# When weight low parts, side work and the modulation stream are issued in a two-layer diffusion backbone on one Trainium2 core

## The chip, the cores and the metric

The kernel runs on one core of a Trainium2 chip. The engines named below are TensorE (PE in the profile; PEld is its weight load), VectorE (DVE), ScalarE (ACT), GpSimd (POOL) and SyncE (SP, which here only issues transfers). The metric is the device time of one execution in microseconds; the median of several runs is given.

## The reference, cut to what matters

One inference step of two layers over 640 tokens of width 1024: 128 context tokens and 512 latent tokens, with the same weights and two modulation vectors.

```python
mod = silu(cond) @ w_ada + b_ada -> shift1, scale1, gate1, shift2, scale2, gate2
h = rmsnorm(x, g_pre_mix) * (1 + scale1) + shift1
z = h @ w_in                       # all branches and their gates
# A: GLU -> depthwise conv 31 -> LayerNorm -> swish;  B: pooling of 2/4/8/16 tokens
# C: b * depthwise conv 3 (c * h);  D: attention of +-128 tokens, latents also read a cache
merged = sum(sigmoid(gate_b) * (branch_b @ w_b_out) for b in "ABCD")
x += gate1 * rmsnorm(merged @ w_o, g_post_mix)
h = rmsnorm(x, g_pre_ffn) * (1 + scale2) + shift2
x += gate2 * rmsnorm(relu(h @ w_ff1)**2 @ w_ff2, g_post_ffn)
```

All is float32. The kernel splits each operand of a large product into a high part that TensorE multiplies fast and a low part (the rest), and sums three products of them.

## The kernel before, in words

The program is written out by Python in one order, and each engine works off its own instructions in that order. TensorE's products give the order its frame; everything else is put between them.

**Weights.** The weights come as 264 units of 128 x 1024, 132 a layer, in the order of use: 6 for q, k, v, 12 for the sections that feed the branches, then the four branches C, B, A, D with their gates (units 18 to 60), 8 for w_o, 64 for the feed-forward part. `w_next` takes the next unit and calls `w_pump` for up to 3 units ahead; `w_done` frees units and pumps again. `w_pump` (L126) issues for a unit the high part on ScalarE (L135), the low part on VectorE (L136), and the transfer of the raw unit three further on (L149, on SP's queue). There are 4 sets of high and low parts and 3 raw buffers.

**Side work.** Attention, branches A, B and C and the modulation are generators (`attention`, `post_a`, `pool_b`, `post_c`, `ada`) that issue a step of work and yield its cost in microseconds of VectorE. After about every half product group the frame calls `tick(pe, dve)` (L70): the TensorE time that has passed, less VectorE's fixed work, is added to a credit with a cap, and each generator in order of its rank gets one step while there is credit. A yield of 0.1 is a lag: a step that issues nothing, so that the next comes a tick later. `drain` issues all that is left of a generator at once. `zsplit` drains a branch before its product begins: C after the first pooling section, B, A and attention inside the last unit of the gates of the branch before.

**Modulation.** `mod_first` makes the first table. The rest is made by `ada`, in chunks of 512 columns: eight pairs of operations on VectorE (L380, L382) that multiply a piece of w_ada by a column of silu(cond) for both vectors, then two all-reductions over partitions on GpSimd (L394). For a gate (2 chunks) the result is multiplied by g_post (L421); for shift and scale (4 chunks) it goes through DRAM into the column tables `mc` (two transfers, L404 and L407), from which `make_ab` makes the tables A and B (L350 to L352). A layer's generator of gate 1 and the second column table is added at the start of its mixer and drained before w_o; that of gate 2 and the next layer's first column table is added before the feed-forward part and drained at the end of it.

**End of a mixer.** `natural` multiplies by w_o in two halves of four units, five token tiles each. In the second half a `Chain` normalises the tiles, adds them to x and makes the next h, with A and B from `ch.start()`. `run` says

```python
self.drain("ada")
ch = Chain(self, f, res[l, "gt1"], xs, lambda t: x1[t], res[l, "ab2"])
ch.start()
self.natural(mhi, mlo, f, "copy", ch)
```

Of the kernel before, what the change touches and what calls it, by code (L numbers as in the profile page):

```python
# [12 lines left out]
L = 2  # L13
# [8 lines left out]
T_BUFS = 26  # L22
# [4 lines left out]
RANK = dict(C=0, B=0, att=1, A=2, ada=3)  # L27
NAT_TICK = ((1.2, 0), (0.9, 0), (0.1, 0), (0.6, 0.6))
FF_DVE = 0.8
KN = {'ws': 0.2, 'l_brow': 2, 'l_red': 2, 'l_red2': 2, 'l_q': 2, 'l_last': 3, 'l_mean': 3, 'l_var': 3, 'l_rb': 4, 'l_ub': 2, 'sec': 0.5, 'gp': 0.1, 'bp': 0.5, 'qs': 2.0, 'qkv': 0, 'j0': -2, 'pv': 0.5, 'sc': 0.5, 'cv': 1.5}  # L30
PE_SCALE, CAP = 1.0, 2.5
W_DVE = 1.2
# [28 lines left out]

class Kernel:
# [19 lines left out]

# [6 lines left out]
    def add(self, name, gen, rank):  # L89
        self.sides.append((rank, name, gen))  # L90
        self.sides.sort(key=lambda s: s[0])

    def drain(self, *names):
        for s in list(self.sides):
            if not names or s[1] in names:
                for _ in s[2]:
                    pass
                self.sides.remove(s)

# [18 lines left out]
    def w_init(self):  # L118
        self.w_dma = 0
        self.w_split = 0  # L120
        self.w_at = 0
        self.w_live = 0
        self.w_raw = {}
        self.w_set = {}

    def w_pump(self, upto):  # L126
        nc = self.nc
        total = L * N_UNITS
        while self.w_split <= min(upto, total - 1) and self.w_live < N_SETS:
            i = self.w_split  # L130
            self.w_fetch(i)
# [4 lines left out]
            nc.vector.tensor_tensor(lo, raw, r32(hi), ALU.subtract)  # L136
            self.credit -= W_DVE
            self.w_set[i] = (hi, lo)
            self.w_split += 1
            self.w_live += 1  # L140
            self.w_fetch(i + N_RAW)

    def w_fetch(self, upto):
        while self.w_dma <= min(upto, L * N_UNITS - 1):
            i = self.w_dma
            if len(self.w_raw) >= N_RAW:
                break
            raw = self.wp.tile([128, 1024], F32, tag="wr", name=self.nm("wr"), bufs=N_RAW)
# [97 lines left out]
    def mod_first(self):  # L246
# [80 lines left out]
        self.w_pump(0)  # L327
        turn(1)
        self.w_pump(1)
        next(norm[0])  # L330
# [5 lines left out]
        self.w_pump(2)  # L336
        self.w_pump(3)
        for i in range(3):
# [24 lines left out]
    def ada_chunk(self, l, ch, red):  # L363
# [5 lines left out]
        for k in range(-3, 8):  # L369
# [13 lines left out]
            yield 1.2  # L383
# [40 lines left out]
    def ada(self, jobs, res):  # L424
        for l, j in jobs:
            if j == "gt1" or j == "gt2":
                G = [self.gpool.tile([128, D], F32, tag=f"G{c}", name=self.nm("G"), bufs=1) for c in range(2)]
                res[l, j] = G
                yield from self.ada_gate(l, 2 if j == "gt1" else 5, G)
            else:  # L430
# [5 lines left out]
                res[l, j] = (mc[0], mc[1], "sh" + n, "sc" + n, "g_pre_mix" if n == "1" else "g_pre_ffn")  # L436
# [91 lines left out]
    def natural(self, hi, lo, f, mode, ch=None):  # L528
# [5 lines left out]
        for n in range(2):  # L534
# [8 lines left out]
            if n == 1 and ch:  # L543
                us = [self.w_next() for _ in range(4)]
                for t in range(NT):
                    ps = self.mmps("nat")
                    for j in range(4):
# [10 lines left out]
                        elif j == 2:  # L558
                            ch.s2b(t - 1)
                    if mode == "add":  # L560
# [4 lines left out]
                self.w_pump(self.w_at + 1)  # L565
                return
# [199 lines left out]
    def post_a(self, us, z):  # L766
        nc = self.nc
        acc = []
        for i in range(2):
# [3 lines left out]
            for k in range(31):  # L773
# [7 lines left out]
                c += 0.8  # L781
# [124 lines left out]
    def mixer(self, l, hi, lo, mhi, mlo):  # L906
# [28 lines left out]
        self.add("att", self.attention(l, kvs, qns), RANK["att"])  # L935

        def section(fn):
            u, st = self.w_next()
            for h in range(2):
# [3 lines left out]
                self.tick(1.63, KN['sec'])  # L943
# [41 lines left out]
        self.add("A", self.post_a(ua, za), RANK["A"])  # L985
# [9 lines left out]
        self.add("C", self.post_c(uc, sb, zc), RANK["C"])  # L995

        ub = []
        for i in range(2):
# [10 lines left out]
            if i == 0:  # L1009
                nz = zsplit("C")  # L1010
        self.add("B", self.pool_b(l, ub, zb), RANK["B"])
# [3 lines left out]
        for bi, br in enumerate("CBAD"):  # L1015
# [3 lines left out]
            for f in range(8):  # L1019
# [9 lines left out]
                for h in range(2):  # L1029
# [7 lines left out]
                    self.tick(1.63, KN['gp'])  # L1037
# [5 lines left out]
                for h in range(2):  # L1043
# [14 lines left out]
                    self.tick(0.41 * nk, KN['bp'])  # L1058
# [4 lines left out]
    def ffn(self, hi, lo, f, ch):  # L1063
        nc = self.nc
        for c in range(4):
# [17 lines left out]
            for i, h in order:  # L1083
# [6 lines left out]
                self.tick(1.63, FF_DVE)  # L1090
# [6 lines left out]
    def run(self):  # L1097
# [3 lines left out]
        with tc.tile_pool(name="cp", bufs=1) as self.cp, tc.tile_pool(name="lp", bufs=1) as self.lp, \  # L1101
# [18 lines left out]
            res = {}  # L1120
            for l in range(L):
                self.layer_tables(l)
                self.add("ada", self.ada([(l, "gt1"), (l, "ab2")], res), RANK["ada"])
# [3 lines left out]
                with tc.tile_pool(name="xp", bufs=1, **SB) as self.xp:  # L1127
                    f = [self.xp.tile([128, D], F32, tag=f"f{t}", name=self.nm("f"), bufs=1) for t in range(NT)]
                    self.drain("ada")
# [3 lines left out]
                    self.natural(mhi, mlo, f, "copy", ch)  # L1133
                    hi, lo = ch.h
                    self.pend = ch.rest(0)
                    f = [self.xp.tile([128, D], F32, tag=f"f{t}", name=self.nm("f"), bufs=1) for t in range(NT)]
                    self.add("ada", self.ada([(l, "gt2")] + ([(l + 1, "ab1")] if l + 1 < L else []), res), RANK["ada"])
                    ch = Chain(self, f, None, lambda t: x1[t], (lambda t: x2[t]) if l + 1 < L else self.x_out, None)

                    def start(ch=ch, l=l):  # L1140
                        self.drain("ada")
                        ch.G = res[l, "gt2"]
                        if l + 1 < L:
                            self.layer_cols(l + 1)
# [4 lines left out]
                    self.ffn(hi, lo, f, ch)  # L1149
                    self.pend = ch.rest(1)  # L1150
# [7 lines left out]
class Chain:  # L1158
# [177 lines left out]
```

## Time and profile before

| | us |
|---|---|
| median of 3 runs | 2117.81 (2117.01 to 2119.41) |
| the profiled execution | 2116.92 |
| its span, first to last instruction | 2115.0 |
| TensorE busy in the span | 2034.1 |
| mean granted clock of TensorE, share of full | 0.984 |

The span is 1.9 us shorter than the execution that it is from. The profile shows one execution: for each engine the time that instructions ran, and for the idle time in front of an instruction what it waited for last. In rows of the timeline the first two numbers are the start and the duration, and brackets hold the idle time before and the instruction that ended it.

### The profile page before, as it was taken

The numbers are of one execution on the slowest core, as the hardware profiler recorded it, in microseconds if no ns is written. First come the engines' busy times: TensorE is split into PE (matmuls) and PEld (weight loads), VectorE is DVE, ScalarE is ACT, GpSimd is POOL, SyncE is SP. The second block draws the span as 40 slices with busy tenths as digits, with TensorE's granted clock in tenths as the row PEclk, the third lists the DMA queues.
The fourth block names the chain that finished last, engine by engine and source line by source line (L and its number), as shares of the span: only waits on it lengthen the run. The fifth ranks groups of instructions, "written<-read, shape, count | busy, mean of one in ns | idle before, by whom it ended". The sixth has DMA issues, their size and how long they took to land.

```text
span 2115.0 us, 30666 instructions
## 1 busy us (share of the span) xinstructions
PE 2034.1 (96%) x12354; PEld 1883.7 (89%) x12354; DVE 1314.5 (62%) x2306; ACT 788.7 (37%) x1540; POOL 283.0 (13%) x214
## 2 busy tenths in 40 slices
PE   8999998999699999999999999999996999999998
PEld 4999997999589898989889989989995989989896
DVE  6668766676677364754476768675784855333344
ACT  5434444442173241313354344454323633323131
POOL 1202000102321012220021020001132211000000
PEclk9999999999899999999999999999998999999999
DMA  8322221233434333332343112222443432222232
GB/s 302 116 69 68 71 67 57 84 110 130 137 143 132 116 120 120 110 120 70 119 140 103 61 64 80 68 84 71 133 132 127 157 118 92 84 78 72 80 100 80
DMA packets 77934, 221.40 MB, mean 105 GB/s; under 512 B 11224, under 2 KB 12248, under 8 KB 77792
## 3 DMA queue, kind: packets, MB, share of 16 engines
q1 hardware_dynamic: 48736, 165.32, 23.0%
q10 hardware_dynamic: 27520, 54.03, 7.7%
q8 instruction: 96, 1.57, 0.3%
q0 software_dynamic: 1536, 0.10, 0.3%
q14 instruction: 46, 0.38, 0.1%
HBM read 208.61 MB, written 10.80 MB: 104 GB/s over the span
## 4 chain that ended last, share of the span: by engine, by line
PE 77%; DVE 11%; ACT 5%; issue 2%; POOL 2%; DMA 2%; SPq 0%; ACTq 0%; DVEq 0%; POOLq 0%
PE nat L174 8%; PE nat L173 8%; PE nat L175 8%; PE ff L178 7%; PE ff L179 7%; PE ff L177 7%; PE gp L177 5%; PE gp L179 5%; PE gp L178 5%; PE sec L177 2%; PE sec L179 2%; PE sec L178 2%; DVE wl L136 2%; DVE cv L780 2%; PE bp L177 1%
## 5 line engine op out<-in xcount | busy, mean ns | idle before, releaser
L136 DVE TENSOR_TENSOR wl<-wr,wh 128x1024 fp32r<-128x1024 f32 x264 | 327.5, 1246 | 321.7 <-ACT wh L135 317.6
L135 ACT CAST wh<-wr 128x1024 fp32r<-128x1024 f32 x264 | 273.4, 1045 | 398.4 <-PE nat L175 282.8
L178 PE MATMUL ff<-hlo,wh 128*128 128x320 f32 x1024 | 317.8, 310 | 3.5 <-DVE hlo L503 3.5
L177 PE MATMUL gp<-hhi,wh 128*128 128x320 f32 x1024 | 320.9, 313 | 0.0
L177 PE MATMUL ff<-hhi,wh 128*128 128x320 f32 x1024 | 318.4, 311 | 0.0
L179 PE MATMUL gp<-hhi,wl 128*128 128x320 f32 x1024 | 317.8, 310 | 0.0
L179 PE MATMUL ff<-hhi,wl 128*128 128x320 f32 x1024 | 317.8, 310 | 0.0
L178 PE MATMUL gp<-hlo,wh 128*128 128x320 f32 x1024 | 317.6, 310 | 0.0
L173 PE MATMUL nat<-wh,ghi 128*128 128x512 f32 x640 | 252.7, 395 | 0.0
L174 PE MATMUL nat<-wl,ghi 128*128 128x512 f32 x640 | 252.5, 395 | 0.0
L175 PE MATMUL nat<-wh,glo 128*128 128x512 f32 x640 | 251.9, 394 | 0.0
L394 POOL PARTITION_ALL_REDUCE red<-acc x40 | 146.9, 3719 | 712.6 <-DVE acc L389 369.0
L382 DVE SCALAR_TENSOR_TENSOR acc<-wa,silu_c,acc 128x512 f32<-128x512 f32 x280 | 193.7, 750 | 7.0 <-DMA wa<-in_wada_dram 7.0
L178 PEld LDWEIGHTS ff<-hlo,wh 128*128 128x128 f32 x1024 | 193.5, 189 | 4.1 <-issue 3.9
L177 PEld LDWEIGHTS gp<-hhi,wh 128*128 128x128 f32 x1024 | 194.0, 189 | 1.6 <-ACT sg L1033 0.2
L178 PEld LDWEIGHTS gp<-hlo,wh 128*128 128x128 f32 x1024 | 193.8, 189 | 1.4
L177 PEld LDWEIGHTS ff<-hhi,wh 128*128 128x128 f32 x1024 | 193.4, 189 | 1.0 <-ACT hhi L500 0.8
L179 PEld LDWEIGHTS gp<-hhi,wl 128*128 128x128 f32 x1024 | 193.5, 189 | 0.0
L179 PEld LDWEIGHTS ff<-hhi,wl 128*128 128x128 f32 x1024 | 193.3, 189 | 0.0
L1076 DVE TENSOR_TENSOR r<-r 128x320 f32<-128x320 f32 x128 | 79.3, 620 | 173.9 <-ACT ghi L1075 173.8
L1074 ACT ACTIVATE r<-ff 128x320 f32<-128x320 f32 x128 | 56.1, 438 | 258.8 <-PE ff L179 251.6
L1033 ACT ACTIVATE sg<-gp 128x320 f32<-128x320 f32 x128 | 55.4, 435 | 252.7 <-PE gp L179 233.2
(205 smaller groups left out, 3798.9 us busy)
## 6 DMA issues: line engine op xcount, KB each, us to landing
wr<-in_wu_dram SPq DMA_DIRECT2D x264, 512.0 KB, 3.3
wa<-in_wada_dram ACTq DMA_DIRECT2D x160, 256.0 KB, 3.1
wa<-in_wada_dram SPq DMA_DIRECT2D x16, 512.0 KB, 8.9
x<-x ACTq DMA_DIRECT2D x15, 512.0 KB, 2.6
x<-x SPq DMA_DIRECT2D x15, 512.0 KB, 5.2
x<-in_x_sample_dram SPq DMA_DIRECT2D x8, 512.0 KB, 7.6
gp<-in_g_post_dram ACTq DMA_DIRECT2D x16, 256.0 KB, 3.1
out_dram<-x SPq DMA_DIRECT2D x10, 256.0 KB, 2.0
```

The costliest lines, as they stand in the source:

```text
L135: nc.scalar.copy(hi, raw)
L136: nc.vector.tensor_tensor(lo, raw, r32(hi), ALU.subtract)
L173: mm(out, lhsT=xhi, rhs=whi, start=start, stop=False)
L174: mm(out, lhsT=xhi, rhs=wlo, start=False, stop=False)
L175: mm(out, lhsT=xlo, rhs=whi, start=False, stop=stop)
L177: mm(out, lhsT=whi, rhs=xhi, start=start, stop=False)
L178: mm(out, lhsT=whi, rhs=xlo, start=False, stop=False)
L179: mm(out, lhsT=wlo, rhs=xhi, start=False, stop=stop)
L382: nc.vector.scalar_tensor_tensor(acc[c], w[k], s, acc[c], ALU.mult, ALU.add)
L394: nc.gpsimd.partition_all_reduce(red[c], acc[c], 128, bass_isa.ReduceOp.add)
L1074: nc.scalar.activation(r, ps[:, :HALF], AF.Relu)
L1076: nc.vector.tensor_tensor(r, r, r, ALU.mult)
```

## The change

1. `w_pump` issues the high part only and puts the unit on a list. `w_low` issues the low part and then the transfer of a further raw unit; it is called with one unit at the end of each tick, at some places of `natural`, and from `w_next` for all up to the unit that is about to be used.
2. A tick goes over the generators in order of slack, that is units until the due unit times 5, less the steps left (`DUE` gives both), and may give a second step to one whose first cost more than a lag. The modulation has no due unit and comes last.
3. Modulation is one generator for both layers, in the order gate 1, columns 2, gate 2 of layer 0, columns 1 and 2 and gates 1 and 2 of layer 1. A gate's chunks wait until the tiles of the gate before are free (`gates`). Where a table is needed, `need` issues the stream up to it.
4. `Chain.start` no longer makes A and B; `late` does, in the second half of `natural` after its four units are taken.
5. C's split moves behind the second pooling section, one more tile buffer is there, and constants change.

```diff
-T_BUFS = 26
+T_BUFS = 27
-RANK = dict(C=0, B=0, att=1, A=2, ada=3)
+DUE = dict(C=(0, 4), B=(0, 24), A=(36, 46), att=(47, 128))
+TICKS = 5
-PE_SCALE, CAP = 1.0, 2.5
-W_DVE = 1.2
+PE_SCALE, CAP = 1.0, 4.0
+W_DVE = 1.15
...
     def tick(self, pe, dve):
         self.credit = min(self.credit + PE_SCALE * pe - dve, CAP)
-        for s in list(self.sides):
-            if self.credit <= 0:
-                break
-            c = 0
-            while c is not None and c < 0.1:
-                c = next(s[2], None)
-            if c is None:
-                self.sides.remove(s)
-            else:
+        again = sorted(self.sides, key=self.slack)
+        for _ in range(2):
+            now, again = again, []
+            for s in now:
+                if self.credit <= 0:
+                    break
+                c = next(s.gen, None)
+                if c is None:
+                    self.sides.remove(s)
+                    continue
                 self.credit -= c
+                s.left -= 1
+                if c > 0.1:
+                    again.append(s)
+        self.w_low(1)
...
+    def slack(self, s):
+        return (s.unit - self.w_at) * TICKS - s.left
...
+    def need(self, *job):
+        while job not in self.res:
+            c = next(self.side_ada.gen, 0)
+            assert c != 0 or job in self.res, job
...
             nc.scalar.copy(hi, raw)
-            nc.vector.tensor_tensor(lo, raw, r32(hi), ALU.subtract)
-            self.credit -= W_DVE
             self.w_set[i] = (hi, lo)
+            self.w_late.append((i, raw, hi, lo))
...
+    def w_low(self, n=None, upto=None):
+        while self.w_late and (n is None or n > 0) and (upto is None or self.w_late[0][0] <= upto):
+            i, raw, hi, lo = self.w_late.pop(0)
+            self.nc.vector.tensor_tensor(lo, raw, r32(hi), ALU.subtract)
+            self.credit -= W_DVE
+            self.w_raw_live -= 1
             self.w_fetch(i + N_RAW)
+            n = None if n is None else n - 1
...
         self.w_pump(i + SPLIT_AHEAD)
+        self.w_low(upto=i)
...
-                self.tick(1.63, KN['ws'])
+                self.tick(1.76, KN['ws'])
...
-            yield 1.2
+            yield 1.4
...
+        jobs = [(0, "gt1"), (0, "ab2"), (0, "gt2"), (1, "ab1"), (1, "ab2"), (1, "gt1"), (1, "gt2")]
         for l, j in jobs:
-            if j == "gt1" or j == "gt2":
+            if j in ("gt1", "gt2"):
+                while self.gates.get((l, j)) is None:
+                    yield 0
...
                 us = [self.w_next() for _ in range(4)]
+                ch.late()
...
-                c += 0.8
+                c += 0.95
...
-            if i == 0:
+            if i == 1:
                 nz = zsplit("C")
...
-                    self.drain("ada")
+                    self.need(l, "gt1")
+                    self.need(l, "ab2")
...
     def start(self):
-        self.A, self.B = self.k.make_ab(*self.ab)
         self.h = self.k.hT()
         self.H = self.k.H
 
+    def late(self):
+        if self.ab:
+            self.A, self.B = self.k.make_ab(*self.ab)
```

Of the constants that VectorE's share of a tick is counted with, `ws` goes from 0.2 to 0.0 and `bp` from 0.5 to 0.75; a branch product counts 0.44 us a block for 0.41.

## Rows read from the trace of the kernel before

**Rows 1.** The page's busy times: us, share of the span, instructions
```profile
PE 2034.1 (96%) x12354; PEld 1883.7 (89%) x12354; DVE 1314.5 (62%) x2306; ACT 788.7 (37%) x1540; POOL 283.0 (13%) x214
```

**Rows 2.** Stages: mixer 0, feed-forward 0, mixer 1; PE, PEld, DVE, ACT, POOL, clock
```profile
75.00:540.00 465.00, 451.44 (x3044) 441.80 (x3043) 328.25 (x639) 191.22 (x392) 52.65 (x39) 0.99 0.26 85
...
625.00:1050.00 425.00, 425.00 (x2393) 386.20 (x2392) 239.66 (x346) 132.32 (x222) 60.89 (x33) 1.00 0.35 113
...
1080.00:1577.00 497.00, 486.11 (x3316) 475.86 (x3315) 354.71 (x680) 206.84 (x426) 60.31 (x46) 0.99 0.28 91
```

**Rows 3.** TensorE's waits: us in total, times, longest
```profile
PE nat L174 <- DVE wl L136: 33.2, 2, 16.7
...
PE rb L818 <- DVE dg L812: 7.8, 2, 6.2
PE PT L696 <- ACT S L685: 6.5, 10, 2.1
...
PE ub L177 <- DVE ot L713: 2.8, 1, 2.8
```

**Rows 4.** Timeline of TensorE: first product with w_o, after layer 0's wait, after layer 1's
```profile
539.59 0.39 PE L173 MATMUL nat<-wh,mh 128*128 128x512 f32 x1
...
577.33 0.80 PE L174 MATMUL nat<-wl,mh 128*128 128x512 f32 x1 [16.49 <-DVE wl L136]
...
1615.13 0.79 PE L174 MATMUL nat<-wl,mh 128*128 128x512 f32 x1 [16.72 <-DVE wl L136]
```

**Rows 5.** The stream's multiply-adds (L382) by stretch of layer 0: VectorE's busy time
```profile
350.00:540.00 190.00, 36.02 (x52) 0.98 0.32 106
540.00:582.00 42.00, 12.18 (x18) 0.80 0.44 138
625.00:950.00 325.00, 57.83 (x84) 1.00 0.37 120
```

**Rows 6.** Timeline of VectorE at the end of layer 0's mixer
```profile
552.38 9.36 DVE L382 SCALAR_TENSOR_TENSOR acc<-wa,silu_c,acc 128x512 f32<-128x512 f32 x14
575.76 0.18 DVE L350 TENSOR_TENSOR A<-mc,cols 128x16 f32<-128x16 f32 x1 [14.02 <-DMA mc<-mrow]
...
576.06 3.49 DVE L136 TENSOR_TENSOR wl<-wr,wh 128x1024 fp32r<-128x1024 f32 x3
```

**Rows 7.** Timeline of GpSimd there
```profile
561.84 6.45 POOL L394 PARTITION_ALL_REDUCE red<-acc  x2 [2.49 <-DVE acc L382]
```

**Rows 8.** Slices of 2 us behind the two long waits; columns as rows 2
```profile
580.00:582.00 2.00, 2.00 (x7) 1.53 (x6) 0.00 (x0) 0.00 (x0) 0.00 (x0) 0.58 0.78 254
...
1618.00:1620.00 2.00, 2.00 (x8) 1.58 (x7) 0.00 (x0) 0.00 (x0) 0.00 (x0) 0.66 0.91 262
```

**Rows 9.** VectorE's waits: us in total, times, longest
```profile
DVE wl L136 <- ACT wh L135: 317.6, 104, 7.9
```

**Rows 10.** Timeline of VectorE and TensorE in layer 0's attention
```profile
317.10 1.23 DVE L136 TENSOR_TENSOR wl<-wr,wh 128x1024 fp32r<-128x1024 f32 x1 [5.00 <-ACT wh L135]
...
319.88 0.33 PE L696 MATMUL PT<-ident,S 128*128 128x128 f32 x1 [2.12 <-ACT S L685]
```

**Rows 11.** Timeline of ScalarE in layer 1's pooling branch
```profile
1232.28 0.72 ACT L198 CAST phi<-pl 128x640 fp32r<-128x640 f32 x1 [8.54 <-POOL pl L870]
```

**Rows 12.** Timeline of one softmax in layer 0
```profile
342.96 0.16 DVE L673 SCALAR_TENSOR_TENSOR neg<-mx,sink 128x4 f32<-128x4 f32 x1
...
349.96 0.72 ACT L685 ACTIVATE S<-S,den 128x512 f32<-128x512 f32 x1 [2.43 <-DVE den L682]
```

**Rows 13.** Timeline of VectorE in layer 1's attention, while GpSimd reduces
```profile
1442.12 2.19 DVE L673 SCALAR_TENSOR_TENSOR neg<-mx,sink 128x4 f32<-128x4 f32 x1
```

More of the change, by code (lines that the diff above doesn't have):

```diff
@@ L59, in r32, with __init__ @@
     return ap.bitcast(F32)
+class Side:
+    def __init__(self, name, gen, unit, left):
+        self.name, self.gen, self.unit, self.left = name, gen, unit, left
 class Kernel:
@@ L87, in next_pend, with add @@
                 fn()
-    def add(self, name, gen, rank):
-        self.sides.append((rank, name, gen))
-        self.sides.sort(key=lambda s: s[0])
+    def slack(self, s):
+        return (s.unit - self.w_at) * TICKS - s.left
+    def add(self, name, gen, unit, steps):
+        self.sides.append(Side(name, gen, self.l * N_UNITS + unit, steps))
     def drain(self, *names):
         for s in list(self.sides):
-            if not names or s[1] in names:
-                for _ in s[2]:
+            if not names or s.name in names:
+                for _ in s.gen:
                     pass
                 self.sides.remove(s)
+    def need(self, *job):
+        while job not in self.res:
+            c = next(self.side_ada.gen, 0)
+            assert c != 0 or job in self.res, job
     def nm(self, p):
@@ L123, in w_init @@
         self.w_raw = {}
+        self.w_raw_live = 0
+        self.w_late = []
         self.w_set = {}
@@ L130, in w_pump @@
             i = self.w_split
+            if i not in self.w_raw:
+                self.w_low()
             self.w_fetch(i)
@@ L145, in w_fetch @@
             i = self.w_dma
-            if len(self.w_raw) >= N_RAW:
+            if self.w_raw_live >= N_RAW:
                 break
+            self.w_raw_live += 1
             raw = self.wp.tile([128, 1024], F32, tag="wr", name=self.nm("wr"), bufs=N_RAW)
@@ L327, in mod_first @@
         self.w_pump(0)
+        self.w_low()
         turn(1)
         self.w_pump(1)
+        self.w_low()
         next(norm[0])
@@ L336, in mod_first @@
         self.w_pump(2)
+        self.w_low()
         self.w_pump(3)
+        self.w_low()
         for i in range(3):
@@ L559, in natural @@
                             ch.s2b(t - 1)
+                        if j % 2:
+                            self.w_low(1)
                     if mode == "add":
@@ L565, in natural @@
                 self.w_pump(self.w_at + 1)
+                self.w_low(1)
                 return
@@ L934, in mixer @@
         self.vt = self.atp.tile([128, 6, 2, 128], F32R, tag="vt", name=self.nm("vt"), bufs=1)
-        self.add("att", self.attention(l, kvs, qns), RANK["att"])
+        self.add("att", self.attention(l, kvs, qns), *DUE["att"])
         def section(fn):
@@ L942, in section @@
                 fn(h, slice(h * HALF, h * HALF + HALF), ps[:, :HALF])
-                self.tick(1.63, KN['sec'])
+                self.tick(1.76, KN['sec'])
             self.w_done(u)
@@ L1036, in mixer @@
                         nc.vector.tensor_tensor(y, y, m_, ALU.add)
-                    self.tick(1.63, KN['gp'])
+                    self.tick(1.76, KN['gp'])
                     if h == 0 and br == "D" and f > 0:
@@ L1057, in mixer @@
                         late.append((macc[f], m))
-                    self.tick(0.41 * nk, KN['bp'])
+                    self.tick(0.44 * nk, KN['bp'])
             self.w_done(*[u[0] for u in bw])
@@ L1089, in ffn @@
                 half(i, h, us[i][1])
-                self.tick(1.63, FF_DVE)
+                self.tick(1.76, FF_DVE)
                 if h == 1:
@@ L1119, in run @@
             self.late_consts()
-            res = {}
+            self.l, self.res, self.gates = 0, {}, {(0, "gt1"): True}
+            self.side_ada = Side("ada", self.ada(), 10000, 0)
+            self.sides.append(self.side_ada)
+            res = self.res
             for l in range(L):
+                self.l = l
                 self.layer_tables(l)
-                self.add("ada", self.ada([(l, "gt1"), (l, "ab2")], res), RANK["ada"])
                 mhi, mlo = [], []
@@ L1133, in run @@
                     self.natural(mhi, mlo, f, "copy", ch)
+                    self.gates[l, "gt2"] = True
                     hi, lo = ch.h
@@ L1149, in run @@
                     self.ffn(hi, lo, f, ch)
+                    self.gates[l + 1, "gt1"] = True
                     self.pend = ch.rest(1)
```

18 lines of the change are left out of this document (9 added, 9 removed).

## Prediction

> **What bounds the kernel now.** I read the busy times first, then a table by stage, then TensorE's waits, and only then single moments. TensorE is busy 96% of the span and VectorE 62% [rows 1]: whatever a change does to VectorE, ScalarE or GpSimd shows only where TensorE waits for it. The span is 2115.0 us and TensorE's busy time 2034.1, so 80.9 us of idle is nearly all there is to win, beside work done at half clock behind an idle stretch. By stage, the feed-forward part of layer 0 has none of it (425.00 busy of 425), and VectorE is at 56% there [rows 2]. The mixer of layer 0 has 465 - 451.4 = 13.6 us, that of layer 1 497 - 486.1 = 10.9 us [rows 2]. The list of TensorE's waits names the largest item: the projection w_o waits for a weight's low part twice, 33.2 us in all [rows 3]. That is 16.49 us at the end of layer 0's mixer and 16.72 us at the end of layer 1's [rows 4].
>
> Why that low part is late can be read on VectorE. At the end of the mixer the modulation stream is drained. Its last 18 multiply-adds lie in this stage [rows 5], the last run of 14 ends at 552.38 + 9.36 = 561.7 [rows 6]. GpSimd then needs 6.45 us for two reductions [rows 7], two small transfers follow, and the column table A, the next instruction in VectorE's order, waits 14.02 us for them. The weight's low part stands behind A in that queue although it needs nothing of it; it runs at 576.06 [rows 6]. TensorE had started the projection at 539.59 and ran out at 577.33 - 16.49 = 560.8 [rows 4], so it had 21.2 us of cover.
>
> The clock makes it dearer. After each of the two idle stretches the granted clock is 0.50, the 1.2 GHz level. In the slice 580 to 582 its mean is 0.58, so half clock lasted 1.68 us into it (2 - x/2 = 1.16), to 581.7; in layer 1 the mean of 0.66 puts the end at 1619.4 [rows 8]. Work ran at half rate for 4.4 and 4.3 us, which lost 2.2 and 2.1 us.
>
> **The change part by part.** *Table A moved behind the weights* (Chain.late). A is now made after four more weight units are issued, half a projection later. With exactly the drain of before, VectorE would finish the multiply-adds at 561.7 and the low part 1.2 us later, about 563, against 560.8 when TensorE runs out: a stall of 2.1 us for 16.5. The reductions and transfers then have half the projection (21.2 us is three units of the four [rows 4]) to land behind, which covers the 14.02 us. So this edit alone removes 14.4 us per layer if the stream is no later than now.
>
> *One stream across layers.* The order becomes gate 1, columns 2 and gate 2 of layer 0, columns 1 and 2 of layer 1, then its gates. A chunk is 14 multiply-adds and 2 first products. Layer 0's mixer needs six chunks as before. Before, 52 multiply-adds ran from 350 to 540, 3.7 chunks, and 18 were left [rows 5]. Now a tick may give two steps to a side instead of one: a column chunk's eight products take four ticks, not eight, so 17 ticks instead of 21 a chunk. I expect 0 to 1 chunk left at the end; by the sentence above one costs 2.1 us; I put 1.0. In the feed-forward part, six chunks (84 multiply-adds) were done by 950 [rows 5], 54 us each, and 100 us up to 1050 stood empty: 1.8 chunks of layer 1's columns 2 move there. That leaves layer 1's mixer with at most 4.2 chunks in place of 6, and one of the 6 was what the drain held: nothing is left to drain. The moved multiply-adds (29 x 0.67 = 19 us) lie under a TensorE that is full; without that cover they would cost 19 us. Term: -(16.5 + 16.7) - (2.2 + 2.1) + 1.0 = -36.5 us.
>
> *Low parts one step behind.* VectorE waits 317.6 us in 104 waits for ScalarE's high part [rows 9]. Nearly all are hidden; where they show is in the mixer. At 317.10 a low part had held VectorE for 5.00 us; the softmax's denominators queued behind it, and TensorE's transpose of the probabilities waited 2.12 us, until 319.88 [rows 10]. Now the denominators go first. All such transposes together wait 6.5 us [rows 3]. The gain lies between 0 (the two-step ticks bring transposes closer to their softmax by one tick) and 6.5; I take 3. The transfer of the next raw weight, issued behind the low part on SP's queue, moves by one tick; three sets of weights ahead hide it, and the 16.5 us stalls show what it is to run dry.
>
> *Side work by slack.* Branch A had third place and was finished by force: TensorE sat idle 6.2 us for the layernorm's diagonal, 7.8 in two places [rows 3]. With a due time of its own, A runs in step with attention; the lags in its text then keep the matrix products away from their sources. Between 0 and 7.8; I take 6, the long one. Branch C's split moves behind one section; it needs no new wait, cost 0, covered by the 3.5 us of a gate's first half.
>
> *Two steps in a tick against it.* The pooling branch issues its GpSimd steps and then a ScalarE copy of the result. ScalarE already waited 8.54 us at one such copy, with everything behind it [rows 11], and TensorE lost 2.8 us on the product after it [rows 3]. Two steps a tick bring the copy nearer by up to one tick, 1.76 us by the code's own figure, in each of four places: 0 to 7 us; I take 3. The stream also puts more reductions beside attention: during one, an operation of 4 columns took 2.19 us instead of 0.16 [rows 12, 13], and the longest waits of a transpose are 2.1 us [rows 3]. For up to three more such pairs, 0 to 3 x (2.03 + 2.1) = 12 us; I take 2, since layer 1 gets two chunks fewer.
>
> The Trainium skill (SBUF — State Buffer, Who interferes with whom) says that a VectorE instruction with two SBUF inputs and a GpSimd instruction that reads SBUF exclude each other, the second one blocking until the first is done. By that rule each of three pairs would hold VectorE through the two reductions, as a rival below has it; the 2.19 us agrees with it for one place.
>
> Retuned constants (1.76 for 1.63, a cap of 4.0 for 2.5) let side work start earlier and come in larger bursts; their price is in the two terms above. The startup, the weights inside the feed-forward parts and the tail keep their order, and the feed-forward part has no idle time to win or lose below its cover of 44% free VectorE: 0.
>
> Sum: -36.5 - 3 - 6 + 3 + 2 = -40.5 us. The profiled run took 2116.92 us; 2076.4. The median of the runs lies 0.9 above that run: **2077 us**.
>
> **The rivals.** *Contention eats the mixer's gain* (0.17): the reductions meet attention in three pairs and more, 12 us instead of 2, and the slack order brings only what it loses; 2077 + 10 = 2087. For it: the 2.19 us. Against: layer 1 loses two chunks from its mixer. *The stream is late in layer 0* (0.10): two chunks or more are left. Each beyond the first is 16 operations of 0.67 us, 10.7 us, straight onto the stall: 2088, with a third 2098. For it: attention, A and the stream share the same ticks. *The mixers' idle time goes* (0.11): the counter terms are nothing, and 14.3 us (both waits whole) to all 24.5 are saved where the sum has 4; 2056 to 2067. *Slower by bursts* (0.06): a softmax needs 7.7 us from its negated maximum at 342.96 to the first scaled row at 350.7 [rows 12]. Before, four ticks lay between it and the transpose; two steps a tick make it three. If the credit never runs out, three ticks in the gate stage are 3 x 8.8/6 = 4.4 us (the code counts 2 x 3.52 and 2 x 0.88 us for a unit's six ticks), so TensorE waits 3.3 us in each of 20 groups, 67 us: 2077 + 67 = 2144. It decides from 2.0 us a group, 40 us in all. Against it: A and the stream drain the credit, and ticks without credit spread the steps. *The drain only moves* (0.03): the wait for A's table reappears before the first modulated tile; 2117.
>
> **How the numbers follow.** Forecast 0.53, own range 2068 to 2086 from the terms taken in part. Rivals as above. The 8-in-10 range reaches from the case without idle in the mixers to a late stream with some contention: 2056 to 2094. Faster, over 0.2% or 4 us, which is about what a measurement of this kernel can tell from no change, holds in the forecast and the first three rivals, 0.91; slower 0.06; the same 0.03.
>
> **What would show it.** The two 16 us waits of the projection gone or under 3 us, no half clock after them; A's three small operations standing behind weight low parts without a wait; some 28 multiply-adds of the stream between 950 and 1080; TensorE's wait for the diagonal gone; VectorE's waits for the high part well under 317 us. Wrong would be: waits of transposes above 40 us in all, waits of the pooling products grown, or a run of multiply-adds still on VectorE when the projection's fourth unit is due.

## The result and the profile after

| | before | after |
|---|---|---|
| median, us | 2117.41 (2116.44 to 2119.41, 4 runs) | 2088.31 (2086.46 to 2092.19, 4 runs) |
| the profiled execution / its span | 2116.92 / 2115.0 | 2086.46 / 2084.5 |
| mean granted clock | 0.984 | 0.991 |

The ratio is 0.9864 [0.9847, 0.9881]: 29 us faster, where 40.5 were forecast. The time lies inside the range (2056 to 2094) and 11 us above the point.

The page's busy times and the three stages (us, then busy time of PE, PEld, DVE, ACT and POOL, granted clock) answer to [rows 1, 2]:

```profile
PE 2031.9 (97%) x12354; PEld 1884.3 (90%) x12354; DVE 1312.2 (63%) x2306; ACT 786.5 (38%) x1540; POOL 287.5 (14%) x214
```
```profile
75.00:540.00 465.00, 455.91 (x3072) 445.32 (x3071) 338.90 (x656) 191.40 (x394) 63.36 (x46) 1.00 0.27 91
625.00:1050.00 425.00, 424.92 (x2352) 382.79 (x2352) 280.08 (x405) 134.17 (x228) 91.43 (x54) 1.00 0.40 133
1080.00:1577.00 497.00, 482.53 (x3250) 470.94 (x3249) 321.48 (x626) 198.66 (x405) 42.98 (x33) 0.99 0.24 81
```

VectorE's work moved as forecast: 40 us more of it lies in the feed-forward part of layer 0 and 33 us less in layer 1's mixer window. But the idle time of TensorE in that window grew, from 10.9 to 14.5 us. TensorE's waits (us in total, times, longest) say on what. In these lines S are attention's scores, PT the transposed probabilities, O the product with V, ub the pooling product, nat a product with w_o or the second feed-forward weight, hT the transpose of a normalised tile:

```profile
PE S L707 <- DVE ot L760: 7.8, 1, 7.8
PE O L755 <- DVE ptl L746: 6.1, 8, 1.7
PE PT L743 <- ACT S L732: 4.5, 12, 1.3
PE qkv L209 <- DVE wl L170: 4.0, 3, 3.2
...
PE O L754 <- ACT pth L745: 1.4, 1, 1.4
```

The 33.2 us of the projection and the 7.8 us of the layernorm's diagonal [rows 3] are gone. New are one wait of 7.8 us for attention's output, one of 3.2 us for a low part at the layer change, and waits of the product with V (O), 7.5 us in all. The two projections now run at full clock from end to end (columns as above):

```profile
536.80:597.20 60.40, 58.74 (x267) 47.45 (x265) 37.35 (x70) 29.23 (x66) 18.69 (x17) 1.00 0.36 136
1564.49:1622.86 58.37, 58.37 (x267) 47.58 (x265) 31.23 (x65) 29.55 (x66) 9.50 (x12) 1.00 0.39 143
```

The end of layer 0's mixer on VectorE, beside [rows 6]: the stream's last products end at 538.5, the projection starts at 536.80, three low parts follow at 546.35, and table A stands behind the last low part and waits for nothing.

```profile
535.80 2.73 DVE L421 SCALAR_TENSOR_TENSOR acc<-wa,silu_c,acc 128x512 f32<-128x512 f32 x4
...
546.35 3.49 DVE L170 TENSOR_TENSOR wl<-wr,wh 128x1024 fp32r<-128x1024 f32 x3
...
568.33 1.23 DVE L170 TENSOR_TENSOR wl<-wr,wh 128x1024 fp32r<-128x1024 f32 x1 [6.18 <-ACT wh L160]
569.47 0.17 DVE L389 TENSOR_TENSOR A<-mc,cols 128x16 f32<-128x16 f32 x1
```

The stream's multiply-adds by stretch (VectorE's busy time and count), beside [rows 5]; the 28 after 950 are those that the prediction moved there:

```profile
350.00:537.00 187.00, 36.77 (x54) 1.00 0.33 108
...
597.00:950.00 353.00, 70.29 (x103) 1.00 0.39 130
950.00:1057.00 107.00, 18.73 (x28) 1.00 0.41 139
```

**Where the time went, by stage.** A stage starts with the first product of its kind in TensorE's timeline (q, k, v; sections; gates and branch products; w_o; feed-forward), so each row below adds up to the span. Columns with a 2 are both layers together; the experiments are told further down.

```
                        start  qkv x2  sec x2  gates0  gates1   w_o 0   w_o 1  ffn x2    span
before                  36.23   98.06  181.74  364.14  362.35   77.13   77.38  917.97  2115.0
after                   37.90  100.16  182.01  359.01  365.66   60.40   58.37  920.99  2084.5
e1_table_late           37.07   97.83  181.75  364.45  361.48   70.71   72.15  918.56  2104.0
e2_table_early          36.42  100.48  181.98  357.30  365.14   68.32   58.31  921.05  2089.0
e3_low_at_once          36.91   97.59  187.81  360.91  363.90   58.49   58.92  918.37  2082.9
e4_low_late_only        36.91  101.28  182.63  360.35  361.00   83.66   83.84  920.83  2130.5
e5_one_step             37.95  101.03  181.68  354.11  352.27   60.16   58.41  921.19  2066.8
e6_pool_one             36.82  100.45  182.00  369.73  364.15   60.24   58.37  921.54  2093.3
e7_stream_by_layer      36.62  100.53  182.50  358.83  366.59   60.39   60.29  921.55  2087.3
e8_low_late_in_mixer    36.83   97.81  183.26  361.40  369.69   60.48   58.54  918.49  2086.5
e9_one_step_low_mixer   36.81   98.01  181.76  352.79  361.23   61.33   58.52  918.45  2068.9
e10_two_steps_stream    37.81   99.43  181.54  368.27  349.60   58.40   58.31  921.14  2074.5
e11_two_steps_chains    36.69   99.63  184.38  358.47  356.87   60.40   58.27  921.29  2076.0
e12_cap_2_5             36.63   99.97  183.25  362.48  368.79   65.16   58.07  921.45  2095.8
```

The two projections gave 16.7 + 19.0 = 35.7 us, the gates 1.8, and 7.1 us came back elsewhere: 1.7 in the startup, 2.1 around q, k, v, 3.0 in the feed-forward parts, 0.3 in the sections. A row is one profile: the changed kernel and `e2_table_early` are the same up to layer 0's projection, and differ by 1.5 us in the startup and by 1.7 in layer 0's gates, so differences of this size in these stages say nothing.

**The new wait of 7.8 us.** VectorE and GpSimd, then TensorE, in layer 1's attention:

```profile
1221.04 8.07 DVE L827 SCALAR_TENSOR_TENSOR cv<-val,wch,cv 128x113 f32<-128x113 f32 x8
...
1231.08 0.69 DVE L760 TENSOR_TENSOR ot<-O,o 64x512 f32<-64x512 f32 x1
...
1233.68 1.89 DVE L827 SCALAR_TENSOR_TENSOR cv<-val,wch,cv 128x117 f32<-128x117 f32 x4
```
```profile
1220.91 1.29 POOL L891 TENSOR_TENSOR s<-up 128x663 f32<-128x663 f32 x1 [2.84 <-PE O L754]
1222.28 1.29 POOL L902 TENSOR_TENSOR s<-s 128x661 f32<-128x661 f32 x1
1224.19 1.29 POOL L905 TENSOR_TENSOR s<-s 128x657 f32<-128x657 f32 x1 [0.63 <-PE ub L214]
1225.57 1.87 POOL L908 TENSOR_TENSOR s<-s 64x649 f32<-64x649 f32 x1
```
```profile
1231.83 0.69 PE L707 MATMUL S<-kt,qt 128*128 128x384 f32 x1 [7.78 <-DVE ot L760]
```

Two steps of branch A's convolution, eight multiply-adds, stand in front of attention's output. They are not a first and a second step of one tick. Worked through tick by tick, the program issues them in two ticks, with one between that has no credit, and gives no side a second step in these. Four of them take 1.89 us with GpSimd idle, at 1233.68; these eight take 8.07 beside the pooling branch's four sums, 4.3 more than twice 1.89. The output waits behind them, two merges and a low part, and the next scores wait for the output. The clock follows: it is 0.50 (1.2 GHz) from 1226 to 1236, so the products behind the wait run at half rate for 4.4 us, which loses 2.2.

```profile
1226.00:1228.00 2.00, 0.00 (x0) 0.00 (x0) 2.00 (x3) 0.00 (x0) 1.43 (x1) 0.50 0.00 0
...
1234.00:1236.00 2.00, 2.00 (x9) 2.00 (x9) 1.57 (x4) 0.00 (x0) 0.00 (x0) 0.50 0.00 0
```

### The profile page after: what moved, and what is told of

It is laid out like the page before. It is cut to its first block, busy times and chain, and to the rows that moved or that the text cites. A ratio compares the mean times of both kernels' runs of the same rounds, so it can differ in the third digit from the quotient of the medians.

```text
span 2084.5 us, 30672 instructions
## 1 busy us (share of the span) xinstructions
PE 2031.9 (97%) x12354; PEld 1884.3 (90%) x12354; DVE 1312.2 (63%) x2306; ACT 786.5 (38%) x1540; POOL 287.5 (14%) x214
## 5 line engine op out<-in xcount | busy, mean ns | idle before, releaser
L170 DVE TENSOR_TENSOR wl<-wr,wh 128x1024 fp32r<-128x1024 f32 x264 | 346.6, 1316 | 211.4 <-ACT wh L160 210.2
L1123 DVE TENSOR_TENSOR r<-r 128x320 f32<-128x320 f32 x128 | 62.6, 489 | 156.7 <-ACT ghi L1122 156.5
```

The costliest lines, as they stand in the source:

```text
L170: self.nc.vector.tensor_tensor(lo, raw, r32(hi), ALU.subtract)
L1123: nc.vector.tensor_tensor(r, r, r, ALU.mult)
```

## The experiments

### The two edits at the projection

`e1_table_late` is the kernel before with only table A moved:

```diff
     def start(self):
-        self.A, self.B = self.k.make_ab(*self.ab)
...
                 us = [self.w_next() for _ in range(4)]
+                ch.late()
```

> The kernel before with one part of the change: table A is made in the second half of the projection, behind its four weight units. Theory 1 (the long waits of the projection came from table A standing ahead of the weights' low parts): both waits fall from 16.5 and 16.7 us to about 2, the half clock behind them goes, 2117 - 33 = 2084 to 2090 us. Theory 2 (the stream itself is late, its multiply-adds and reductions hold VectorE): the waits stay above 10 us each, 2105 to 2117.

Measured: 2105.91 us, ratio 0.994 [0.9928, 0.9953]. TensorE's timeline in layer 0 shows a stall of 2.07 us for 16.49, the prediction's 2.1. But the projection became only 6.4 us shorter in layer 0 and 5.2 in layer 1. TensorE's waits and VectorE's timeline say why:

```profile
563.86 0.50 PE L174 MATMUL nat<-wl,mh 128*128 128x512 f32 x1 [2.07 <-DVE wl L136]
```
```profile
PE hT L474 <- ACT xn L458: 14.6, 3, 7.1
...
PE nat L174 <- DVE wl L136: 5.1, 2, 3.0
```
```profile
559.27 3.40 DVE L382 SCALAR_TENSOR_TENSOR acc<-wa,silu_c,acc 128x512 f32<-128x512 f32 x5
...
569.42 3.06 DVE L136 TENSOR_TENSOR wl<-wr,wh 128x1024 fp32r<-128x1024 f32 x1 [3.35 <-ACT wh L135]
572.80 1.23 DVE L136 TENSOR_TENSOR wl<-wr,wh 128x1024 fp32r<-128x1024 f32 x1 [0.32 <-ACT wh L135]
581.00 0.18 DVE L350 TENSOR_TENSOR A<-mc,cols 128x16 f32<-128x16 f32 x1 [6.98 <-DMA mc<-mrow]
```
```profile
562.77 9.62 POOL L394 PARTITION_ALL_REDUCE red<-acc  x2 [2.43 <-DVE acc L382]
```

The multiply-adds end at 562.7, the queue reaches A after the last low part at 574.0, and A's table lands at 581.0: 18.3 us were needed and 11.3 were there. Nor do the reductions stay as they were: the low parts now run beside them, and they take 9.62 us for 6.45 [rows 7], while one of the low parts takes 3.06 us for 1.23. Behind A on VectorE stand small operations on the sums of squares and the scalings of the first tiles, and TensorE waits for the normalised tile instead. The waits that theory 1 names are gone, but the time is that of theory 2: the wait moved, and of the two projections' 33.2 us 11.6 were won.

`e2_table_early` is the mirror: the changed kernel with `make_ab` back in `start`.

> The changed kernel with table A back in front of the projection. Its stream ended in time, so theory 1 expects in layer 0 a wait only as long as the last reductions and transfers (they end some 10 us after the projection begins, inside its 21 us of cover) and none in layer 1: 2088 to 2092. Theory 2 (the late table does the work, the stream across layers brings little): one or both 16 us waits come back, 2103 to 2120.

Measured: 2093.1 us, 0.9877 [0.9864, 0.9891]. The projection takes 68.3 us in layer 0, where A waits again, and 58.3 in layer 1, where nothing is left to wait for:

```profile
553.59 0.17 DVE L389 TENSOR_TENSOR A<-mc,cols 128x16 f32<-128x16 f32 x1 [10.05 <-DMA mc<-mrow]
```

So without the late table the changed kernel, whose stream ends earlier, gives 8.8 us in layer 0 and all of the 19 in layer 1; the late table is worth a further 8 us in layer 0 once the stream ends in time. Neither edit replaces the other in layer 0.

`e7_stream_by_layer` takes the work of layer 1's columns 2 out of layer 0's feed-forward part:

```diff
-(1, "ab1"), (1, "ab2"), (1, "gt1"), (1, "gt2")]
+(1, "ab1"), (1, "gt1"), (1, "ab2"), (1, "gt2")]
```

> The changed kernel, but layer 1's second columns wait for its first gate, so its stream has to do six chunks inside its own mixer, as before. Theory 1 (work across layers is what empties layer 1's drain): layer 1's projection grows from 58 to about 65 to 72 us, total 2095 to 2103. Theory 2 (the faster ticks alone get six chunks done): 2085 to 2092.

Measured: 2092.81 us, 0.9873 [0.9859, 0.9888]. Layer 1's projection takes 60.3 us for 58.4. The faster pace of the stream inside the mixer finishes nearly in time by itself; giving it work across the layers is worth 2 us in that stage, and by the ratios, 0.9873 for 0.9864, the two kernels can't be told apart.

### The low parts one step behind

`e4_low_late_only` is the kernel before with `w_low` alone:

```diff
-            nc.vector.tensor_tensor(lo, raw, r32(hi), ALU.subtract)
+            self.w_late.append((i, raw, hi, lo))
...
     def tick(self, pe, dve):
+        self.w_low(1)
```

> The kernel before with low parts one step behind and nothing else. Theory 1: the two 16 us waits stay, and 0 to 5 us come from the transposes in the mixers, 2110 to 2118. Theory 2: 2095 to 2107.

Measured: 2132.45 us, 1.006 [1.0048, 1.0073], slower. The gates win 3.8 and 1.4 us, but each projection loses 6.5. TensorE's timeline after layer 0's wait:

```profile
573.78 0.80 PE L189 MATMUL nat<-wl,mh 128*128 128x512 f32 x1 [22.67 <-DVE wl L150]
```

One more unit's low part is still on the list when the drain and A are issued, so it stands behind A. TensorE ran out at 573.78 - 22.67 = 551.1, 14.3 us after the projection's start at 536.8, two units of work where there were three (21.2 us). What the prediction hoped for did come in the gates: TensorE's waits for transposes and products with V are 2.4 us in this run, 6.8 in the kernel before.

`e3_low_at_once` undoes it in the changed kernel (`self.w_low()` right after the list is filled).

> The changed kernel with each low part issued right behind its high part again; all else as changed. Theory 1 (low parts one step behind pay little: VectorE's long waits for high parts are hidden by TensorE): 2084 to 2094, VectorE's wait for high parts back near 300 us. Theory 2 (they free VectorE in the mixers): waits of the transposes and of the attention products grow, 2098 to 2115.

Measured: 2088.04 us, 0.9856 [0.9841, 0.9871]: the same time. The sections lose 5.8 us, the gates together nothing; q, k, v win 2.6 and the feed-forward parts 2.6. VectorE's waits for the high part, 317.6 us before [rows 9], are 210.2 in the changed kernel and 362.2 here, and the time does not follow them (VectorE's waits of the changed kernel, then of this one):

```profile
DVE wl L170 <- ACT wh L160: 210.2, 59, 6.2
```
```profile
DVE wl L171 <- ACT wh L160: 362.2, 123, 11.3
```

`e8_low_late_in_mixer` keeps the step only between a mixer's first section and its last gate:

```diff
             self.w_late.append((i, raw, hi, lo))
+            if self.low_now:
+                self.w_low()
```

> The changed kernel with low parts one step behind only in the sections and gates of the mixer, at once elsewhere. The stages of the two kernels say that the delay gains some 6 us in the sections and loses about as much where a normalised tile and a low part follow each other at the layer changes. Theory 1 (the two are independent and cancel): 2080 to 2085. Rival (the sections' gain was chance of one profile): 2086 to 2091.

Measured: 2090.37 us, 0.9864 [0.9849, 0.9879]. What was lost at the layer change and in the feed-forward parts came back (2.4 and 2.5 us), and the gates became 2.4 and 4.0 longer, with one new wait of 7.6 us of the pooling product for its ScalarE copy. The gates answer to any shift of the steps.

### One step a tick, and which steps collide

`e5_one_step` changes one number of the changed kernel:

```diff
-        for _ in range(2):
+        for _ in range(1):
```

> The changed kernel with one step per generator and tick instead of two. Theory 1 (two steps a tick build bursts that TensorE waits for, the 7.8 us of layer 1 among them): both gate stages get shorter by 2 to 6 us together, but the stream may end later in layer 0, so the projections may lose up to 8; 2080 to 2094. Theory 2 (the second step is what lets the stream end in time): projection of layer 0 loses 10 us and more, 2098 or above.

Measured: 2067.74 us (2065.57 to 2069.79), 0.9757 [0.9742, 0.9771]: 20.6 us faster than the changed kernel and faster than either theory, with the projections as short as there. The stream did not need the second step: 14 multiply-adds, a whole chunk, are left for layer 0's projection where two steps leave 3, but the low parts come right behind them, ahead of A, and TensorE waits only 1.50 us (VectorE, then TensorE):

```profile
540.17 5.39 DVE L421 SCALAR_TENSOR_TENSOR acc<-wa,silu_c,acc 128x512 f32<-128x512 f32 x8 [2.20 <-DMA wa<-in_wada_dram]
```
```profile
546.75 0.50 PE L209 MATMUL nat<-wl,mh 128*128 128x512 f32 x1 [1.50 <-DVE wl L170]
```

The gains are 4.9 and 13.4 us in the two gate stages. The windows of both gate stages (the changed kernel, then this one; length, then PE's busy time):

```profile
177.79:536.80 359.01, 349.92 (x2321) 340.05 (x2319) 264.03 (x485) 149.59 (x287) 50.49 (x33) 1.00 0.26 87
1198.83:1564.49 365.66, 351.19 (x2324) 342.09 (x2324) 232.22 (x441) 153.04 (x302) 30.13 (x17) 0.98 0.21 70
```
```profile
176.75:530.86 354.11, 348.07 (x2325) 340.24 (x2323) 259.17 (x478) 151.18 (x288) 50.64 (x33) 1.00 0.28 89
1194.40:1546.67 352.27, 348.29 (x2325) 340.26 (x2323) 242.38 (x456) 152.48 (x300) 40.05 (x23) 1.00 0.24 79
```

TensorE's idle time there falls from 9.1 + 14.5 = 23.6 us to 6.0 + 4.0 = 10.0, and its busy time by 4.7, of which 2.2 are the half clock behind the wait of 7.8 us; the rest is not explained. In the kernel before the idle time was 13.6 + 10.9 = 24.5 [rows 2]. Two groups of waits make up the difference. The wait for attention's output is 1.0 us for 7.8, and transposes and products with V together wait 3.7 us, where it is 12.0 in the changed kernel and 6.8 in the kernel before (TensorE's waits of this run):

```profile
PE PT L743 <- ACT S L732: 1.7, 8, 0.3
...
PE O L755 <- DVE ptl L746: 1.5, 2, 1.0
```

Runs of eight multiply-adds are there with one step a tick too, from two ticks behind each other. The collision itself is still there (VectorE's timeline of this run):

```profile
1201.38 3.67 DVE L827 SCALAR_TENSOR_TENSOR cv<-val,wch,cv 128x116 f32<-128x116 f32 x8
...
1215.36 1.88 DVE L827 SCALAR_TENSOR_TENSOR cv<-val,wch,cv 128x113 f32<-128x113 f32 x4
...
1220.48 4.28 DVE L827 SCALAR_TENSOR_TENSOR cv<-val,wch,cv 128x115 f32<-128x115 f32 x4
```

Four multiply-adds beside the sums take 4.28 us for 1.88. But only four stand there, and attention's output went ahead at 1213.50. All 240 of these operations take 119.2 us on VectorE in the kernel before, in the changed one and here: the slowing by the sums is as large in each, and what stands behind it differs.

`e6_pool_one` was to give the pooling branch one step a tick: its GpSimd steps cost 0.1 instead of 0.11, so that no second step follows.

> The changed kernel with the pooling branch's GpSimd steps at one a tick (their cost 0.1 instead of 0.11); all else two. Theory 1 (the 7.8 us wait of layer 1 comes from GpSimd's sums running beside a burst of eight convolution steps on VectorE): that wait goes or shrinks under 3 us, layer 1's gate stage 366 to about 356 to 360 us, total 2078 to 2086. Rival: the burst of eight alone does it, the wait stays above 5 us, 2086 to 2091.

Measured: 2095.9 us, 0.9894 [0.9878, 0.9911]. The wait of 7.8 us stays as it was and layer 0's gates grow by 10.7. This does not test the pace of the pooling steps. Worked through tick by tick, the changed kernel gives 105 second steps, 67 to the modulation, 35 to attention, 3 to branch A and none to pooling, so the edit had none to take away. All that it changes is 0.01 us of credit per step, and with it the tick that some steps fall in. What it does show is how far placement alone can move a gate stage: by 10.7 us.

Three of the last four kernels ask which second step costs. `e10_two_steps_stream` lets only the modulation have one, `e11_two_steps_chains` only attention and the branches:

```diff
-                if c > 0.1:
+                if c > 0.1 and s.name == "ada":
```

> The changed kernel where only the modulation stream may take a second step in a tick; attention and the branches take one. Theory (the second step costs because it brings a chain's step closer to the one it depends on): the stream's multiply-adds depend on nothing recent, so the gates stay near 354 and 352 and the time near 2068 us. Rival (it costs because two steps' work on VectorE stand in one tick ahead of the gate's own multiply, whichever side they are from): the gates stay near 359 and 366 and the time near 2088 us.

> The mirror of it: attention and the branches may take a second step in a tick, the stream only one. Theory (a chain's steps come too close): near 2088 us, with the wait for attention's output of some 8 us or others like it in the gates. Rival (load of a tick, mostly the stream's): near 2068 us. If both this one and its mirror lie near 2078, the cost is shared.

Measured: 2076.18 us (0.9798 [0.9785, 0.9812]) and 2081.62 us (0.9823 [0.9809, 0.9836]). Both gate stages together take 706.4 us with no second step, 717.9 with the stream's, 715.3 with the chains', 724.7 with both. Neither theory held alone. A shared cost would look like this, but the differences are no larger than what placement alone did in `e6_pool_one`, so it is not shown. Nor does it lie evenly: the stream's costs 14.2 us in layer 0 and gains 2.7 in layer 1. In layer 0 about a third of it is again one place (VectorE, GpSimd and TensorE of `e10_two_steps_stream`):

```profile
199.06 5.32 DVE L827 SCALAR_TENSOR_TENSOR cv<-val,wch,cv 128x113 f32<-128x113 f32 x4
...
206.24 0.99 DVE L931 TENSOR_SCALAR ub<-ub,cols 128x320 f32<-128x320 f32 x2
```
```profile
199.17 1.37 POOL L902 TENSOR_TENSOR s<-s 128x661 f32<-128x661 f32 x1 [0.49 <-PE ub L213]
200.62 1.60 POOL L905 TENSOR_TENSOR s<-s 128x657 f32<-128x657 f32 x1
202.30 1.55 POOL L908 TENSOR_TENSOR s<-s 64x649 f32<-64x649 f32 x1
```
```profile
206.83 0.69 PE L707 MATMUL S<-kt,qt 128*128 128x384 f32 x1 [5.08 <-DVE ub L931]
```

Here one convolution step is enough, 5.32 us for four, since the pooling branch's scaling, for which TensorE waits, stands behind it.

`e12_cap_2_5` puts the cap on saved credit back (`CAP` 2.5 for 4.0), two steps kept.

> The changed kernel with the cap on saved credit back at 2.5 us, two steps a tick kept. Theory (bursts need saved credit, and the higher cap feeds them): a good part of the 20 us of the second step comes back, about 2075 us. Rival (credit seldom reaches 2.5 us, as the sides always have work): no change, 2088 us.

Measured: 2098.48 us, 0.9906 [0.9893, 0.992], 10 us slower than the changed kernel, which neither theory had. Layer 0's stream ends later (its projection takes 65.2 us for 60.4), and the gates grow by 6.6 us, with two new single waits: 7.8 us of the pooling product for its ScalarE copy, and 5.0 of the scores for the pooling branch's scaling.

`e9_one_step_low_mixer` joins `e5_one_step` and `e8_low_late_in_mixer`.

> The changed kernel with one step a tick, and with low parts one step behind only in the mixer's sections and gates, at once elsewhere. Theory (the two edits act in different stages, so their gains add): the layer change goes from 53.1 to 48.9 us and the two feed-forward stages lose 1.6 and 0.9 us, as they did with two steps a tick, while the gate stages stay at 354 and 352; 2067.7 - 6.7 = 2061 us. Rival (what is won at the layer change is given back in the gates, as it was with two steps a tick): 2068 us with the gates of layer 1 some 4 us longer.

Measured: 2071.79 us (2069.67 to 2073.66), 0.9779 [0.9765, 0.9792]. The stages in which the low parts had cost something win as forecast (3.0 and 2.7 us), and layer 1's gates grow by 9.0, 5.3 of it one wait of the pooling product for its ScalarE copy. The rival held. The best version measured is `e5_one_step`.

## Why the prediction was right, and where it was not

The kernel came out 10 us above the sum by the profile: 0.8 of them lie in the projections, 2.2 in the gates and 7.1 in stages that the prediction put at 0.

- **The projections: right in size, wrong in what does it.** The two waits and the half clock behind them are gone; the stages gave 35.7 us for the 36.5 of that term, and A stands behind the low parts without a wait. The step that failed is "this edit alone removes 14.4 us per layer". The late table removes the stall (2.07 measured for 2.1), but the prediction gave A half a projection of cover, 21.2 us, where the queue is past the last of the four low parts 11.3 us after the multiply-adds end, and the reductions and transfers, counted at 14.02, took 18.3 beside those low parts. What was left of the wait became TensorE's wait for the normalised tile, and `e1_table_late` gave 6.4 and 5.2 us. The stream that ends earlier does more: without the late table it gives 8.8 and 19. That two steps a tick are what ends it in time did not hold either: `e5_one_step` leaves a whole chunk for layer 0's projection, which the prediction priced at 2.1 us and which costs a wait of 1.5, and that projection takes 60.2 us for 60.4.
- **Low parts one step behind: the 3 us came where they were looked for and were lost elsewhere.** On the kernel before, transposes and products with V wait 2.4 us for 6.8, and the gates gain 5.1. But in all the edit costs 0.6% there, about 13 us, because it puts one more unit behind A; this the prediction did not look for. In the changed kernel it wins in the sections what it loses at the layer changes and in the feed-forward parts. The prediction's "startup, the weights inside the feed-forward parts and the tail keep their order: 0" failed here: about 5 of the 7.1 us given back are these, since `e3_low_at_once` and `e8_low_late_in_mixer` recover them. The 1.7 us of the startup are not explained; kernels with the same startup took 36.4 to 38.0 us.
- **Branch A by slack: the wait went, the time did not.** The diagonal's 7.8 us is gone, yet TensorE's idle time in the gates went only from 24.5 to 23.6 us, as other waits took its place.
- **Two steps in a tick: right in sign, too small by far.** The prediction counted 3 us, for a pooling copy that comes too early. The second step costs 20.6 us in the median and 18.3 in the gate stages. The place it named was not the one: pooling takes no second step, and no copy of it holds TensorE in the changed kernel (in `e8_low_late_in_mixer`, `e9_one_step_low_mixer` and `e12_cap_2_5` one does, for 7.6, 5.3 and 7.8 us). TensorE's idle time in the gates is 13.6 us more with the second step. Of this 8.3 are attention's chain, transposes and products with V, and 6.8 the wait for its output, less 1.5 in smaller waits the other way. The rival on the slower side came near the first: it had the right edit and the right chain, one link too early (transposes fell from 6.5 to 4.5 us, products with V rose from 0 to 7.5), and held three times as much in all. The changed kernel and the six others that let both the modulation and attention take a second step wait 10.2 to 16.9 us in that chain, take 722 to 734 us in the gate stages and 2088 to 2098 in all; the two with one step wait 3.7 and 5.0 and take 706 and 714, and 2068 and 2072 in all. So it is shown that the second step costs; how much of the 20.6 us is its own is not, since placement alone moves a stage by 10.
- **The mixer's sum was therefore nearly right from two wrong terms.** It had -9 for low parts and order and +5 against them, -4 in all, where the gates gave -1.8. With one step a tick the same edits give 20.1 us, and the second step takes 18.3 of them back. On the kernel before, the low parts alone gave 5.1 in the gates (`e4_low_late_only`); if that adds up, the other 15 are order and constants, which were not tried apart.
- **Reductions beside attention.** Three of TensorE's waits over 0.8 us in the gate stages come within 4 us after a GpSimd reduction, 0.93, 1.42 and 1.65 us: at most 4.0 where the term had 2. So the rival of 2087, at which the time nearly came out, is not what happened, and its nearness is luck. The row that spoke for it was also read too strongly: the operation of 2.19 us ended at 1444.31 [rows 13], while the two reductions ran to 1448.55, and another with two inputs in SBUF took 0.16 us in between, so this pair did not hold VectorE through, as the prediction reads the rule that it cites:

```profile
1441.73 6.82 POOL L394 PARTITION_ALL_REDUCE red<-acc  x2 [52.45 <-DVE acc L389]
```
```profile
1444.55 0.16 DVE L675 TENSOR_TENSOR es<-neg,sink 128x4 f32<-128x4 f32 x1
```

What stays open: why a second step, mostly the modulation's and attention's, lengthens attention's chain, and why a given placement meets the collision of convolution and sums. The gate stages lie between 706 and 734 us over these kernels, and most of the longer ones show one or two single waits of 4 to 8 us, in other places each time. But `e3_low_at_once` has none above 3.8 us and is as long as the changed kernel (724.8 for 724.7), so the collision is not the whole cost. No run held the convolution away from the sums.

## What to carry to other kernels

When a wait is moved behind other work, ask what is queued behind it in its new place, and count cover only from there. Judge a scheduler by what it puts in front of each instruction that the bounding engine waits for, not by the total of the side work: that total can stay the same to a tenth of a microsecond while the span moves by one per cent. Before an edit is read as a test of a cause, work through whether it takes that cause away; `e6_pool_one` did not, and showed instead what a harmless shift of the order costs. A term that is a sum of a gain and a counter-gain should be tested with the one undone, since a nearly right sum can hide a much better version.

## What the runs showed of the hardware

VectorE's multiply-adds with two inputs in SBUF, beside GpSimd's sums of 128 x 650 elements or so, lose most of the time that the sums take: four took 1.88 us alone and 4.28 or 5.32 beside them, eight 8.07. The Trainium skill (SBUF — State Buffer, Who interferes with whom) says that such an instruction and a GpSimd instruction that reads SBUF exclude each other. The trace nearly agrees: eight alone are 3.8 us and the four sums 5.7, 9.5 one after the other, and the place lasted from 1220.91 to 1229.11, 8.2 us, so by the profile some of it did overlap.

Two all-reductions over partitions on GpSimd took 6.45 us at the end of layer 0's mixer in the kernel before, and 9.62 us in `e1_table_late`, where VectorE made low parts beside them.

A single idle stretch of TensorE of 7.8 us brought the granted clock to 0.50 before the stretch was over, and it stayed there for 4.4 us of work behind it, as long as the 4.4 and 4.3 us behind the 16 us waits of the kernel before [rows 8].
